# Sums on VectorE instead of GpSimd, four output chunks closed singly, and small matmuls planned later

## The chip, the cores and the metric

One core of one Trainium2 chip runs the whole program in one launch. The metric is device time in microseconds (us). The kernel before took 1167.01 us (median of 3 runs, 1165.86 to 1167.97). PE is the matmul engine (TensorE), DVE is VectorE, ACT is ScalarE, POOL is GpSimd, SP is the queue from which the weights are fetched.

## The reference, cut to what matters

The input is 256 tokens by 1024 features. Two transformer layers and one recurrent layer follow each other.

```python
for i in range(2):                                   # first_block
    h = x * (1.0 + sc_m) + sh_m                      # sc, sh, g: from c @ w_mod
    y = even_mixer(h, ...) if i == 0 else odd_mixer(h, ...)   # q, k: rotary; then out-projection
    x = layer_norm(ALPHA * x + (1.0 + g_m) * y, ln_mix_g[i], ln_mix_b[i])
    h = x * (1.0 + sc_f) + sh_f
    y = swiglu(h, w_gate[i], w_up[i], w_down[i])
    x = layer_norm(ALPHA * x + (1.0 + g_f) * y, ln_ffn_g[i], ln_ffn_b[i])
# second_block: rmsnorm, input projection, gated recurrence, out-projection,
# rmsnorm, convolved gated FFN, final rmsnorm
```

`layer_norm` needs the mean and the mean square over the 1024 features, `rmsnorm` the mean square. `apply_rope` is `t1*cos - t2*sin, t2*cos + t1*sin` on the two halves of each head. The even mixer has two kinds of attention, one of which first selects the 64 best keys of every query (`top_k`); the odd mixer is differential attention.

## The kernel before

**Layout.** Features lie on the 128 partitions, so an activation is 8 chunks of 128 x 256 (feature x token). Every weight is fetched in slabs of 128 x 2048 from SP's queue into `stage`. Each half of a slab (128 x 1024, one output chunk over all 8 input chunks) is rounded by ACT into `whi`, and DVE writes the rest `wlo = stage - whi`. An output chunk is then 8 x 3 matmuls of 128 x 256 (`mm3`): hi*hi, hi*lo, lo*hi. There are 6 buffers each of `whi` and `wlo`, and 8 PSUM banks.

**Order of the work.** Every instruction is recorded first (`Plan.record`) with an estimated cost, its dependences, and its place in the program (plus a bias) as its priority. `Plan.order` then plays the program through: on each engine it takes the ready instruction with the lowest priority number, where an instruction is ready when its inputs are, plus a hop of 300 ns if the input comes from another engine. The result is a fixed order on each engine, which the chip follows; an engine waits at an instruction whose input is late, and everything behind it waits too. The estimates for DVE and POOL don't depend on what the other one does.

**Layer norm over partitions** (`Norm`, used four times). `Norm.add(k, y)` takes output chunk k of a projection: DVE makes the residual `d` from PSUM, ACT and DVE make the split product `U[k]` (the input of the next projection, with the norm applied afterwards), ACT makes `sq = d*d`. POOL adds `d` and `sq` into two running totals s1 and s2 for k below `cut`. From k = cut on, the totals and then every single `d` and `sq` are summed over partitions by `column`: two f32 matmuls of one column each (one for each 128 tokens) against a vector of 1/1024. Each f32 matmul shows in the trace as two records. After k = 7 a few small DVE and ACT steps form the reciprocal root, and `spread` turns the two numbers of each token into a full 128 x 256 tile through four transposes on PE. The next projection's first four chunks (`group(norm.U, ..., outer=True)`, 96 matmuls over k in the outer loop) use `U`, so PE has them to do while the statistics are formed; the later chunks use `X`, which `ln_next` makes from the finished statistics (`ln_next`: two DVE steps, two ACT steps and one DVE step for each of the 8 chunks).

The norms behind the two mixers have cut=4, those behind the FFNs have cut=7. The fourth norm also carries three more totals (`add_sq`). `Rms` is the same with squares alone, twice in the last layer.

**Out-projection** (`out_proj`). It makes chunks 0 to 3 as one group with k in the outer loop, then the four `Norm.add`; then chunks 4 to 7 as a second group, one chunk behind the other, and then their four `Norm.add`.

**Rotary** (`rope_parts`). ACT copies the swapped quarters out of PSUM, DVE multiplies by the cosines, POOL multiplies the swapped copy by the signed sines, DVE adds.

Of the kernel before, what the change touches and what calls it, by code (L numbers as in the profile page):

```python
# [18 lines left out]
S = 256  # L19
# [29 lines left out]
for _l in range(2):  # L49
    for _p in (0, 3):  # L50
        MOD_ORDER += [(_l, _p + i, k) for k in range(8) for i in range(2)]
        MOD_ORDER += [(_l, _p + 2, k) for k in range(8)]

LAG = 300
XLAG = 600
BIAS = {'topk': 75, 'dsa': 75, 'sb': 0, 'diff': 0, 'diffo': -275, 'hgrn': 75, 'fetch': 0}
# [48 lines left out]
class Plan:  # L105
# [26 lines left out]
    def __init__(self, nc):  # L132
        self.ops = []
        self.hist = {}
        self.tiles = {}
        self.bufs = {}
        self.form = {}
        self.spare = {}
        self.bias = 0
        self.nc = nc  # L140
        self.vector = Plan.Engine(self, "DVE", nc.vector)
        self.scalar = Plan.Engine(self, "ACT", nc.scalar)
        self.gpsimd = Plan.Engine(self, "POOL", nc.gpsimd)
        self.tensor = Plan.Engine(self, "PE", nc.tensor)
        self.sync = Plan.Engine(self, "SP", nc.sync)
        self.aq = Plan.Engine(self, "AQ", nc.scalar)
        self.pq = Plan.Engine(self, "PQ", nc.gpsimd)
# [61 lines left out]
    def record(self, eng, op, fn, args, kw):  # L209
        writes, reads = [], []  # L210
        for i, a in enumerate(args):
            if isinstance(a, View):
                (writes if i == 0 else reads).append(a)
        for k, a in kw.items():
            if isinstance(a, View):
                (writes if k in ("out", "accum_out") else reads).append(a)
        idx = len(self.ops)
        deps = set()
        mine = []
        for lst, w in ((reads, False), (writes, True)):  # L220
            for a in lst:
                name = a.name
                b = self.box(a.sample)
                if self.tiles[name][1] is None:
                    assert w, (op, name)
                    self.tiles[name][1] = idx
                if idx not in self.tiles[name][2][-1:]:
                    self.tiles[name][2].append(idx)
                if name not in mine:
                    mine.append(name)  # L230
                h = self.hist.setdefault(name, [])
                keep = []
                for e in h:
                    j, ew, eb = e
                    over = eb[0] < b[1] and b[0] < eb[1] and eb[2] < b[3] and b[2] < eb[3]
                    if over and (w or ew) and j != idx:
                        deps.add(j)
                    if not (w and b[0] <= eb[0] and eb[1] <= b[1] and b[2] <= eb[2] and eb[3] <= b[3]):
                        keep.append(e)
                keep.append((idx, w, b))  # L240
                self.hist[name] = keep
        cost = self.cost(eng, op, [a.sample for a in writes], [a.sample for a in reads])
        need = self.SETS.get(args[2]) if op == "activation" else None
        work = 0.0
        if eng == "PE":
            work = 1.0
            for v in writes[0].shape[1:]:
                work *= v
            work *= reads[0].shape[0] / 128
            work *= 4 if reads[0].dtype == F32 and op == "matmul" else 2 if op == "transpose" else 1  # L250
        parts = 2 if len(writes) > 1 and eng == "ACT" or eng == "PE" and op == "matmul" and reads[0].dtype == F32 else 1
        self.ops.append((eng, fn, args, kw, cost, deps, mine, idx + self.bias, need, work, parts))

    def order(self):
        import heapq
        ops = self.ops
        n = len(ops)
# [26 lines left out]
        at = [0.0] * n  # L284
# [14 lines left out]
        while done < n:  # L299
            moved = False  # L300
            nxt = float("inf")
            for e in engs:
# [91 lines left out]
                        heapq.heappush(tags[self.tiles[nm][0]]["free"], (last[nm] + 100.0, slot[nm]))  # L394
                for j in succ[i]:
                    oj = ops[j]
                    at[j] = max(at[j], end + (self.SELF[e] if oj[0] == e else self.HOP))
                    need[j] -= 1
                    if not need[j]:
                        heapq.heappush(wait[oj[0]], (at[j], oj[7], j))  # L400
# [31 lines left out]
def kernel(ctx, tc, io, out):  # L432
# [269 lines left out]
    class Norm:  # L702
# [13 lines left out]
        def add(self, k, y):  # L716
            d = self.d[k]
            V.scalar_tensor_tensor(d, y, self.g1[:, k:k + 1], self.xa[k], op0=ALU.mult, op1=ALU.add)
            scale_split(self.U[0][k][:, :S], self.U[1][k][:, :S], d, self.lv[:, 16 + k:17 + k])
            sq = w1("lnq")[:, :S]  # L720
            A.activation(sq, d, AF.Square)
            if k == 0:
                self.q0 = sq
            elif k == 1:
                self.s1 = w1("lns1")[:, :S]
                self.s2 = w1("lns2")[:, :S]
                G.tensor_add(self.s1, self.d[0], d)
                G.tensor_add(self.s2, self.q0, sq)
            elif k < self.cut:
                G.tensor_add(self.s1, self.s1, d)  # L730
                G.tensor_add(self.s2, self.s2, sq)
            if self.sq:
                self.add_sq(k, d)
            if k >= self.cut:
                if k == self.cut:
                    self.p = bank("ps_s")
                    self.column(0, self.s1, first=True)
                    self.column(1, self.s2)
                self.column(0, d, last=k == 7)
                self.column(1, sq, last=k == 7)  # L740
            if k == 7:
                p = self.p
                if self.sq:
                    for c, a in enumerate((self.s3, self.s4, self.s5)):
                        self.column(2 + c, a, last=True)
                st = sm("st", 8)
                V.tensor_copy(st[:, 0:4], p[:, 0:4])
                V.tensor_mul(st[:, 4:6], st[:, 0:2], st[:, 0:2])
                V.tensor_sub(st[:, 4:6], st[:, 2:4], st[:, 4:6])
                root(st[:, 4:6], LN_EPS)  # L750
                V.tensor_mul(st[:, 6:8], st[:, 4:6], st[:, 0:2])
                self.r, self.mr = [bank("ps_b")[:, :S] for _ in range(2)]
                self.spread(self.r, st[:, 4:6])
                self.spread(self.mr, st[:, 6:8])
                self.rm = w2("rm")
                if self.sq:
                    self.root_sq(p[:, 4:10], st)
# [5 lines left out]
                         start=first and t == 0, stop=last, skip_group_check=True)  # L763

        def spread(self, dst, col):
            for t in range(2):
                T.transpose(dst[:, t * 128:t * 128 + 128], col[:, t:t + 1].to_broadcast([128, 128]), ident)

        def add_sq(self, k, d):

            g, gg, gb = [v[:, k:k + 1] for v in self.sq[:3]]
            sq = w1("lnq3")[:, :S]
            A.activation(sq, d, AF.Square, scale=g)
            if k == 0:
                self.q3 = sq
                self.s4 = w1("lns4")[:, :S]
                self.s5 = w1("lns5")[:, :S]
                V.tensor_scalar(self.s4, d, gg, None, op0=ALU.mult)
                V.tensor_scalar(self.s5, d, gb, None, op0=ALU.mult)
                return  # L780
            V.scalar_tensor_tensor(self.s4, d, gg, self.s4, op0=ALU.mult, op1=ALU.add)
            V.scalar_tensor_tensor(self.s5, d, gb, self.s5, op0=ALU.mult, op1=ALU.add)
            if k == 1:
                self.s3 = w1("lns3")[:, :S]
                G.tensor_add(self.s3, self.q3, sq)
            else:
                G.tensor_add(self.s3, self.s3, sq)

        def root_sq(self, p, st):

# [105 lines left out]
    def rope_parts(ps, n):  # L896
# [4 lines left out]
            s = q ^ 1  # L901
            A.activation(rot[q * 32:q * 32 + 32], ps[s * 32:s * 32 + 32], AF.Copy)
        V.tensor_mul(t1, ps, cosT[:, None, :].to_broadcast([128, n, S]))
        G.tensor_mul(rot, rot, sinT[:, None, :].to_broadcast([128, n, S]))
        return t1, rot


# [266 lines left out]
    mod_upto(40, LAG)  # L1174

    def out_proj(O, norm, korder):
        for s in range(2):
            pss = group(O, [ALLT] * 4, korder, outer=s == 0)
            for c in range(4):
                norm.add(4 * s + c, pss[c])  # L1180

    lv = ln_vectors(0, "lmg", "lmb", MV(0, 4, 0, 8), MV(0, 3, 0, 8))
    norm = Norm(xa, MV(0, 2, 0, 8), lv, cut=4)
    out_proj(O, norm, KORDER)

    def ffn_act(Gp, j, gate, up, bias=None):
# [134 lines left out]
    mod_upto(88, LAG)  # L1321

    lv = ln_vectors(1, "lmg", "lmb", MV(1, 4, 0, 8), MV(1, 3, 0, 8))
    norm = Norm(xa, MV(1, 2, 0, 8), lv, cut=4)
    out_proj(O, norm, ALLK)
    Gp, xa = ffn(norm, lv, 96)

# [46 lines left out]
    class Rms:  # L1374
# [7 lines left out]
        def add(self, h):  # L1382
# [7 lines left out]
            if i == 0:  # L1390
                self.acc = sq
            elif i == 1:
                a = w1("racc")[:, :n]
                G.tensor_add(a, self.acc, sq)
                self.acc = a
            elif i < self.cut:
                G.tensor_add(self.acc, self.acc, sq)
            if i >= self.cut:
                if i == self.cut:
                    self.p = bank("ps_s")  # L1400
# [459 lines left out]
```

## Time and profile before

| | |
|---|---|
| median of 3 runs | 1167.01 us |
| the profiled execution | 1165.6 us |
| its span, first to last instruction | 1163.8 us |
| PE busy | 1132.3 us, 97% |
| DVE busy | 910.6 us, 78% |
| ACT busy | 723.5 us, 62% |
| POOL busy | 88.2 us, 8% |
| mean granted PE clock | 0.988 |

The profiled execution lies 1.4 us under the median of the runs; 1.8 us of it lie outside the span. Matmuls overlap in the array, so the duration of one record (some 0.28 us) is longer than the distance from one start to the next (some 0.12 us for 256 columns); costs on PE are read from starts. All recorded instructions carry the same line, L428, since one helper issues them; they are told apart by their tiles: `pa` is PSUM, `w` any work tile, `cst` the constants, `sm` the small tiles, `mst` the modulation weights.

### The profile page before, as it was taken

Reading aid. Unit: us, or ns where it says so; the run is one execution under the profiler, and the core shown is the slowest. Engines: PE = TensorE matmul, PEld = TensorE weight load, DVE = VectorE, ACT = ScalarE, POOL = GpSimd, SP = SyncE. Lnnn points to the kernel's source line nnn. Section 1 sums busy time; section 2 is a strip of 40 time slices with the busy share of each in tenths; the row PEclk is TensorE's granted clock in tenths of the full one; section 3 lists DMA queues with packets and bytes.
Section 4 is the critical chain, followed back from the end, with each engine's and each line's share of the span. In section 5 each row is a group of like instructions: output and inputs, shape, how many; then the busy total and the mean of one; then the engine's idle time right before and its main releaser. Section 6 shows DMA issues by size and latency. Waiting matters only on the chain.

```text
span 1163.8 us, 22183 instructions
## 1 busy us (share of the span) xinstructions
PE 1132.3 (97%) x8835; PEld 1083.9 (93%) x8835; DVE 910.6 (78%) x1686; ACT 723.5 (62%) x1312; POOL 88.2 (8%) x84
## 2 busy tenths in 40 slices
PE   5999999999999899999999999999999999999997
PEld 4885899999999778999999999999999999999996
DVE  6799899888999999865557886996669887866642
ACT  3558676445449887764455558786767865655541
POOL 0110200000231302000003400000000010000011
PEclk9999989999999999899999999999999999999998
DMA  9938758988995333455554634344433424555441
GB/s 353 409 131 309 240 196 319 337 325 305 335 335 191 114 129 126 145 218 184 187 191 168 228 110 158 130 148 179 155 117 131 178 87 171 195 188 193 169 163 37
DMA packets 42247, 232.28 MB, mean 200 GB/s; under 512 B 4640, under 2 KB 6176, under 8 KB 24096
## 3 DMA queue, kind: packets, MB, share of 16 engines
q1 hardware_dynamic: 42144, 230.87, 55.0%
q8 instruction: 69, 1.13, 0.4%
q14 instruction: 34, 0.28, 0.1%
HBM read 229.81 MB, written 1.05 MB: 198 GB/s over the span
## 4 chain that ended last, share of the span: by engine, by line
PE 85%; DVE 7%; DMA 3%; ACT 3%; issue 1%; DVEq 0%; SPq 0%; ACTq 0%
PE pa L428 85%; DVE w L428 4%; ACT w L428 2%; DVE wlo L428 2%; DMA mst<-in_wmod_dram 1%; DVE sm L428 1%; DVE mst L428 1%; DMA whi<-in_w_dram 1%; DMA cst<-in_cst_dram 1%; ACT whi L428 1%; DMA vec<-in_vecs_dram 0%; ACT sm L428 0%; ACT scb L428 0%; DVE lnv0lmg L428 0%; DVEq L1856 0%
## 5 line engine op out<-in xcount | busy, mean ns | idle before, releaser
L428 PE MATMUL pa<-w,whi 128*128 128x256 f32 (+4 forms) x5104 | 914.5, 287 | 9.6 <-DMA whi<-in_w_dram 7.5
L428 PEld LDWEIGHTS pa<-w,whi 128*128 128x128 f32 x5104 | 766.9, 190 | 17.0 <-ACT w L428 7.6
L428 PE MATMUL pa<-w,wlo 128*128 128x256 f32 (+3 forms) x2608 | 659.5, 289 | 0.0
L428 ACT ACTIVATE whi<-stage 128x1024 fp32r<-128x1024 f32 (+1 forms) x330 | 340.2, 1042 | 257.2 <-PE pa L428 233.9
L428 DVE TENSOR_TENSOR wlo<-stage,whi 128x1024 fp32r<-128x1024 f32 (+1 forms) x330 | 401.4, 1226 | 110.1 <-ACT whi L428 104.5
L428 PEld LDWEIGHTS pa<-w,wlo 128*128 128x128 f32 x2608 | 464.0, 190 | 7.7 <-issue 4.0
L428 ACT ACTIVATE w<-w 128x256 fp32r<-128x256 f32 (+9 forms) x257 | 117.6, 470 | 74.0 <-DVE w L428 70.3
L428 ACT ACTIVATE w<-pa 128x256 f32<-128x256 f32 (+12 forms) x298 | 108.3, 391 | 40.9 <-PE pa L428 36.1
L428 DVE TENSOR_TENSOR w<-w,w 128x256 fp32r<-128x256 f32 (+7 forms) x263 | 120.1, 474 | 8.0 <-ACT w L428 5.1
L428 DVE SCALAR_TENSOR_TENSOR mst<-mst,scb 128x1024 f32<-128x1024 f32 x90 | 109.5, 1226 | 10.8 <-DMA mst<-in_wmod_dram 10.6
L428 DVE TENSOR_TENSOR w<-w,pa 128x256 f32<-128x256 f32 (+2 forms) x146 | 58.9, 417 | 57.3 <-PE pa L428 52.3
L428 POOL TENSOR_TENSOR w<-w,w 128x256 f32<-128x256 f32 (+1 forms) x50 | 56.5, 1150 | 527.5 <-ACT w L428 320.7
L427 ACT ACT_TABLE_LOAD x59 | 75.7, 1283 | 1.7 <-PEq L1850 0.7
L428 PE MATMUL pa<-w,w 128*128 128x128 f32 (+8 forms) x340 | 70.0, 331 | 1.7 <-DVE w L428 1.1
L428 PEld LDWEIGHTS pa<-w,w 128*128 128x128 f32 (+4 forms) x340 | 41.4, 171 | 11.5 <-issue 4.1
L428 PE MATMUL pa<-cst,w 128*128 128x1 f32 (+4 forms) x284 | 46.5, 265 | 3.6 <-DVE w L428 2.2
L428 PEld LDWEIGHTS pa<-cst,w 128*128 128x128 f32 (+2 forms) x284 | 36.0, 175 | 12.0 <-ACT w L428 4.5
L428 POOL TENSOR_TENSOR w<-w 128x256 f32<-128x256 f32 x4 | 3.2, 799 | 415.2 <-DVE w L428 415.2
L428 PE MATMUL pa<-w 128*128 128x128 f32 x240 | 34.6, 274 | 0.0
L428 PE MATMUL pa<-whi,w 128*128 128x512 f32 x96 | 32.5, 417 | 0.2 <-ACT w L428 0.2
L428 PEld LDWEIGHTS pa<-w 128*128 128x128 f32 x240 | 31.2, 191 | 0.0
L428 DVE SCALAR_TENSOR_TENSOR w<-pa,vec,w 128x256 f32<-128x256 f32 (+1 forms) x48 | 23.1, 482 | 6.7 <-PE pa L428 5.7
(145 smaller groups left out, 537.1 us busy)
## 6 DMA issues: line engine op xcount, KB each, us to landing
mst<-in_wmod_dram SPq DMA_DIRECT2D x90, 512.0 KB, 5.4
stage<-in_wgu_dram SPq DMA_DIRECT2D x44, 1024.0 KB, 4.9
stage<-in_wi_dram SPq DMA_DIRECT2D x36, 1024.0 KB, 4.8
stage<-in_wup_dram SPq DMA_DIRECT2D x22, 1024.0 KB, 4.8
stage<-in_wd_dram SPq DMA_DIRECT2D x24, 896.0 KB, 4.7
stage<-in_w_dram SPq DMA_DIRECT2D x15, 1024.0 KB, 6.2
stage<-in_wo_dram SPq DMA_DIRECT2D x12, 1024.0 KB, 4.8
stage<-in_wd_dram SPq DMA_DIRECT2D x12, 1024.0 KB, 4.8
```

The source lines that it names most:

```text
L427: self.nc.scalar.preload_act_table_set(tables[i])
L428: fn(*[real(a) for a in args], **{k: real(a) for k, a in kw.items()})
```

## The change

It has five parts.

1. The running totals of `Norm` (s1, s2, and s3 in `add_sq`) and of `Rms` are added on VectorE (`V`) instead of GpSimd (`G`), and so is the sine product of `rope_parts`.
2. The norms behind the mixers get the default cut=7: the totals run over k = 0 to 6, and only k = 7 is summed by itself.
3. In `Norm.add` the column sums of the totals, and of the three extra totals, are recorded at k = 7, ahead of those of `d` and `sq`.
4. `out_proj` still makes chunks 0 to 3 as a group; chunks 4 to 7 are made one at a time, each followed by its own `Norm.add`.
5. A constant HOLD = 800 ns: while `Norm` records column sums or the transposes of `spread`, the planner takes inputs from another engine to be 800 ns later than otherwise. This alters the planned order only; no wait is added to the program itself.

```diff
+HOLD = 800.0
@@ Plan.record
+        if self.hold:
+            self.late[idx] = self.hold
@@ Plan.order
-                    at[j] = max(at[j], end + (self.SELF[e] if oj[0] == e else self.HOP))
+                    at[j] = max(at[j], end + (self.SELF[e] if oj[0] == e else self.HOP + self.late.get(j, 0.0)))
@@ Norm.add
-                G.tensor_add(self.s1, self.d[0], d)
-                G.tensor_add(self.s2, self.q0, sq)
+                V.tensor_add(self.s1, self.d[0], d)
+                V.tensor_add(self.s2, self.q0, sq)
             elif k < self.cut:
-                G.tensor_add(self.s1, self.s1, d)
-                G.tensor_add(self.s2, self.s2, sq)
+                V.tensor_add(self.s1, self.s1, d)
+                V.tensor_add(self.s2, self.s2, sq)
...
             if k >= self.cut:
+                run.hold = HOLD
                 if k == self.cut:
                     self.p = bank("ps_s")
-                    self.column(0, self.s1, first=True)
+                if k == 7:
+                    self.column(0, self.s1, first=self.cut == 7)
                     self.column(1, self.s2)
-                self.column(0, d, last=k == 7)
+                    if self.sq:
+                        for c, a in enumerate((self.s3, self.s4, self.s5)):
+                            self.column(2 + c, a, last=True)
+                self.column(0, d, first=k == self.cut < 7, last=k == 7)
                 self.column(1, sq, last=k == 7)
+                run.hold = 0.0
@@ Norm.spread
+            run.hold = HOLD
             for t in range(2):
                 T.transpose(dst[:, t * 128:t * 128 + 128], col[:, t:t + 1].to_broadcast([128, 128]), ident)
+            run.hold = 0.0
@@ Norm.add_sq (twice) and Rms.add (twice): G.tensor_add becomes V.tensor_add
...
@@ rope_parts
-        G.tensor_mul(rot, rot, sinT[:, None, :].to_broadcast([128, n, S]))
+        V.tensor_mul(rot, rot, sinT[:, None, :].to_broadcast([128, n, S]))
@@ out_proj
-        for s in range(2):
-            pss = group(O, [ALLT] * 4, korder, outer=s == 0)
-            for c in range(4):
-                norm.add(4 * s + c, pss[c])
+        pss = group(O, [ALLT] * 4, korder, outer=True)
+        for c in range(4):
+            norm.add(c, pss[c])
+        for c in range(4, 8):
+            norm.add(c, group(O, [ALLT], korder)[0])
@@ both mixers' norms
-    norm = Norm(xa, MV(0, 2, 0, 8), lv, cut=4)
+    norm = Norm(xa, MV(0, 2, 0, 8), lv)
```

## Rows read from the trace of the kernel before

**Rows 1.** The page: the span, and busy time, share and instructions of three engines.
```profile
span 1163.8 us, 22183 instructions
PE 1132.3 (97%) x8835; PEld 1083.9 (93%) x8835; DVE 910.6 (78%) x1686; ACT 723.5 (62%) x1312; POOL 88.2 (8%) x84
```

**Rows 2.** Whole-run waits of PE: for whom, us in total, times, longest us.
```profile
PE pa L428 <- ACT w L428: 3.8, 9, 1.4
PE pa L428 <- DVE w L428: 3.7, 5, 1.6
...
PE pa L428 <- DVE biasb L428: 1.9, 1, 1.9
PE pa L428 <- DVE sm L428: 1.8, 2, 1.1
```

**Rows 3.** Timeline of PE, first mixer's norm: start, us, what, [idle before].
```profile
148.61 4.55 PE L428 MATMUL pa<-cst,w 128*128 128x1 f32 x40
...
157.05 1.11 PE L428 MATMUL pa<-cst,sm 128*128 128x128 f32 x4 [1.08 <-DVE sm L428]
...
168.87 0.40 PE L428 MATMUL pa<-w,whi 128*128 128x256 f32 x2
```

**Rows 4.** Timeline of PE, second mixer's norm.
```profile
469.12 6.55 PE L428 MATMUL pa<-cst,w 128*128 128x1 f32 x40
...
490.22 0.40 PE L428 MATMUL pa<-w,whi 128*128 128x256 f32 x2
```

**Rows 5.** Windows: us, busy (x) of PE, PEld, DVE, ACT, POOL; PEclk; DMA.
```profile
155.00:160.00 5.00, 3.92 (x19) 3.62 (x19) 4.72 (x16) 2.98 (x6) 0.00 (x0) 0.50 0.86 290
...
345.00:350.00 5.00, 5.00 (x44) 5.00 (x44) 4.90 (x11) 2.47 (x5) 0.00 (x0) 1.00 0.89 324
...
475.00:480.00 5.00, 5.00 (x25) 5.00 (x25) 1.90 (x9) 2.29 (x5) 0.00 (x0) 0.50 0.76 313
```

**Rows 6.** Chain of waits: start, us, what; one unbroken piece on PE.
```profile
853.62 300.46 PE pa L428 x2496
```

**Rows 7.** Timeline of PE at the first FFN's norm (cut=7).
```profile
344.64 0.95 PE L428 MATMUL pa<-cst,w 128*128 128x1 f32 x8
...
346.58 0.50 PE L428 MATMUL pa<-cst,w 128*128 128x1 f32 x4
```

**Rows 8.** Groups by shape, whole run: count | busy us, mean ns | idle before.
```profile
L428 POOL TENSOR_TENSOR w<-w,w 128x256 f32<-128x256 f32 x47 | 53.3, 1156 | 248.1 <-issue 159.0 <-DVE w L428 47.6 <-ACT w L428 41.5
...
L428 DVE TENSOR_TENSOR w<-w,w 128x512 f32<-128x512 f32 x49 | 32.6, 686 | 1.4 <-ACT w L428 1.4
...
L428 DVE TENSOR_TENSOR w<-w,w 128x256 f32<-128x256 f32 x42 | 17.4, 430 | 0.7 <-ACT w L428 0.2
...
L428 POOL TENSOR_TENSOR w<-w,sinT 128x512 f32<-128x512 f32 x9 | 12.7, 1409 | 53.2 <-ACT w L428 45.7 <-DVE w L428 7.6
...
L428 POOL TENSOR_TENSOR w<-w,sinT 128x256 f32<-128x256 f32 x5 | 5.4, 1074 | 54.6 <-ACT w L428 54.5
```

**Rows 9.** Groups on DVE by shape, 137.5 to 146 us, POOL adding beside it.
```profile
L428 DVE TENSOR_TENSOR wlo<-stage,whi 128x1024 fp32r<-128x1024 f32 x3 | 4.2, 1397 | 0.0
L428 DVE SCALAR_TENSOR_TENSOR w<-w,lnv0lmg,w 128x256 fp32r<-128x256 f32 x4 | 3.7, 960 | 0.0
L428 DVE SCALAR_TENSOR_TENSOR w<-pa,mod,w 128x256 f32<-128x256 f32 x4 | 1.7, 478 | 0.0
```

**Rows 10.** The same groups, 149 to 155 us, POOL idle.
```profile
L428 DVE TENSOR_TENSOR wlo<-stage,whi 128x1024 fp32r<-128x1024 f32 x3 | 3.6, 1207 | 0.0
L428 DVE SCALAR_TENSOR_TENSOR w<-w,lnv0lmg,w 128x256 fp32r<-128x256 f32 x4 | 1.9, 468 | 0.0
```

**Rows 11.** Windows, columns as in Rows 5: first out-projection's end; differential attention.
```profile
137.00:149.00 12.00, 12.00 (x105) 12.00 (x103) 12.00 (x17) 9.34 (x18) 6.74 (x6) 1.00 0.47 155
...
365.00:412.00 47.00, 42.94 (x296) 36.32 (x294) 44.90 (x87) 42.91 (x96) 13.95 (x11) 1.00 0.38 135
```

**Rows 12.** Timeline of PE behind the fourth norm.
```profile
685.68 0.50 PE L428 MATMUL pa<-w,whi 128*128 128x258 f32 x2 [0.25 <-ACT w L428]
```

More of the change, by code (lines that the diff above doesn't have):

```diff
@@ L139, in __init__ @@
         self.bias = 0
+        self.hold = 0.0
+        self.late = {}
         self.nc = nc
@@ L734, in add @@
             if k >= self.cut:
+                run.hold = HOLD
                 if k == self.cut:
                     self.p = bank("ps_s")
-                    self.column(0, self.s1, first=True)
+                if k == 7:
+                    self.column(0, self.s1, first=self.cut == 7)
                     self.column(1, self.s2)
-                self.column(0, d, last=k == 7)
+                    if self.sq:
+                        for c, a in enumerate((self.s3, self.s4, self.s5)):
+                            self.column(2 + c, a, last=True)
+                self.column(0, d, first=k == self.cut < 7, last=k == 7)
                 self.column(1, sq, last=k == 7)
+                run.hold = 0.0
             if k == 7:
                 p = self.p
-                if self.sq:
-                    for c, a in enumerate((self.s3, self.s4, self.s5)):
-                        self.column(2 + c, a, last=True)
                 st = sm("st", 8)
@@ L784, in add_sq @@
                 self.s3 = w1("lns3")[:, :S]
-                G.tensor_add(self.s3, self.q3, sq)
+                V.tensor_add(self.s3, self.q3, sq)
             else:
-                G.tensor_add(self.s3, self.s3, sq)
+                V.tensor_add(self.s3, self.s3, sq)
         def root_sq(self, p, st):
@@ L1323 @@
     lv = ln_vectors(1, "lmg", "lmb", MV(1, 4, 0, 8), MV(1, 3, 0, 8))
-    norm = Norm(xa, MV(1, 2, 0, 8), lv, cut=4)
+    norm = Norm(xa, MV(1, 2, 0, 8), lv)
     out_proj(O, norm, ALLK)
@@ L1393, in add @@
                 a = w1("racc")[:, :n]
-                G.tensor_add(a, self.acc, sq)
+                V.tensor_add(a, self.acc, sq)
                 self.acc = a
             elif i < self.cut:
-                G.tensor_add(self.acc, self.acc, sq)
+                V.tensor_add(self.acc, self.acc, sq)
             if i >= self.cut:
```

## Prediction

> **What bounds the kernel now.** I read the page first. PE is busy for 1132.3 of 1163.8 us, DVE for 910.6 [rows 1]; so time is won where PE stands still, runs slowly, or does work that can go, and the rest of the program can at best be hidden. PE's waits come second [rows 2]: those that ACT or DVE end add up to 3.8 + 3.7 + 1.9 + 1.8 = 11.2 us, a third of the 31.5 us that PE is idle; the reader is to see that no single wait is large. Third, PE's timeline at the two norms behind the mixers, since the diff takes PE work away there. From the end of the out-projection PE does 40 column records in one burst, then 96 matmuls of the next projection with four transpose records among them. That takes 148.61 to 168.87, 20.26 us, in the first layer [rows 3], and 469.12 to 490.22, 21.10 us, in the second [rows 4]. The windows show why it is so long: after the burst the granted clock is 0.50, the lower of the two levels (1.2 against 2.4 GHz) [rows 5]. In an undisturbed piece PE starts a matmul every 300.46 / 2496 = 0.120 us [rows 6], so the 96 need 11.5 us at the full clock.
>
> **The change part by part.** The sum is made against the profiled execution, 1165.6 us, which is 1.4 us under the median.
>
> *Column sums.* With cut=4 each mixer norm has (2 + 8) columns of two token halves, each two records: 40, as the rows show. With cut=7 there are 4 x 2 x 2 = 16. The 24 that go cost 4.55 / 40 = 0.114 us each in the first layer, 2.7 us; in the second, where the clock falls during the burst, 6.55 / 40 = 0.164 us.
>
> *The clock behind them.* An FFN norm has 16 records already, in pieces of 8, 4 and 4 with matmuls between [rows 7], and the clock stays at 1.00 around them [rows 5]. I therefore take the mixer norms to keep the full clock as well. Each stretch then needs 16 x 0.114 = 1.8, four transpose records at half of their slow-clock 1.11, say 0.6, and 11.5 us: 13.9. Against 20.26 and 21.10 that is 6.3 and 7.2 us less, in which the 1.08 us wait before the first norm's transposes is included: the later place in the order puts some 0.8 / 0.12 = 7 matmuls into it. What bounds it: the columns alone (2.7 each) if the slow clock comes back, the whole if nothing is late.
>
> *Sums on DVE.* POOL's sums number 45 of the 47 [rows 8], plus four first ones and three of 258 columns; 52 move, and the two mixer norms get six more each. At 0.43 us each, the 64 put 27.5 us on DVE, and the 14 sine products 9 x 0.69 + 5 x 0.43 = 8.4 us: 35.9 in all. Against that stands what POOL does to DVE now. While POOL adds, the split product takes 960 ns and `wlo` 1397 [rows 9]; a few us later, with POOL idle, the same two take 468 and 1207 [rows 10]. Four of the one and three of the other are 2.0 + 0.6 = 2.6 us lost beside six sums, 0.43 for each: as much as the sum will cost on DVE. So I count the moved sums at nothing and only the new ones, 6 x 0.43 = 2.6 us in each mixer norm.
>
> In [rows 9] the product that reads PSUM does not suffer: 478 ns beside POOL. The Trainium skill, "SBUF — State Buffer", section "Who interferes with whom", has the same line: a VectorE instruction with two SBUF inputs and a GpSimd instruction that reads SBUF block each other outright. By that rule the exchange is even, and the trace agrees.
>
> *Who waits for the new sums.* In the first layer DVE is full at that place, 12.00 of 12 us [rows 11], so the transposes, at 157.05 now, can come 2.6 later, at 159.7. From there to the first normalised chunk there are five steps of DVE and ACT, at 0.43 to 0.69 us like the rows of their size: 161.9 to 163.2. PE is through its 96 matmuls at 148.61 + 13.9 = 162.5. Behind the first chunk each of the others follows in three DVE steps, 1.3 us, while PE needs 12 x 0.120 = 1.4. I charge 1.0 us here (bounds 0 and 2.6), nothing in the second layer, where DVE is busy for only 1.90 of the 5 us from 475 [rows 5]. So the norms give -5.3 and -7.2.
>
> *Chunks 4 to 7 singly.* PE's matmuls are the same in number and in order. What moves are the `Norm.add` of chunks 4 to 6, ahead of the fetches and `wlo` splits of the next weights in priority; SP's queue keeps its order. Six buffers each of `whi` and `wlo` hold two chunks in reserve, 2 x 24 x 0.120 = 5.8 us of PE. A `wlo` of 1.2 us that stands behind two more sums is 0.9 us late: hidden, 0; without the reserve it would be 0.9 for each of three chunks.
>
> *Sine products.* In differential attention DVE is busy for 44.90 of 47 us and PE idle for 47 - 42.94 = 4.1 [rows 11]. Ten products fall there, six long and four short: 5.8 us. POOL time cost DVE 2.6 / (6 x 1.156) = 0.37 us per us above; ten products of 1.409 and 1.074 are 12.8 us of POOL, so 4.7 come back: +1.1 net. Each product itself ends earlier, 0.69 for 1.41. Between all idle gone (-4.1) and the net load in full (+1.1) I take the middle, -1.5; the outer bound is +5.8, no relief. The first mixer has the other four, 2.5 us on DVE with 2.0 back, ahead of the key selection for which PE waits 1.9 [rows 2]: I take 0 (bounds -1.9 and +2.5).
>
> *The planned delay.* PE does other matmuls meanwhile, 96 of them at each norm. Only behind the fourth norm is the cover seen to end: PE waits 0.25 us for a normalised chunk [rows 12]. Columns, transposes and the extra transposes may each come 0.8 later; I charge one, +0.8 (bounds 0 and 2.4). `Rms` is not delayed, and its sums move at no price like the others.
>
> Sum: -5.3 - 7.2 - 1.5 + 0 + 0.8 = -13.2; 1152.4 for this execution, 1153.8 beside the median.
>
> **The rivals.** *The slow clock stays.* The order is fixed, and the two totals are now the last sums of a full DVE; if they come later than planned, PE stands at their columns with the 96 matmuls behind it, and the stretch ends slow again. For it: DVE has no idle time at 137 to 149. Against it: POOL's slowing of DVE, which the planner didn't know, goes, so its times fit better. Then only columns are saved, 2 x 2.7 less the 0.8: 1165.6 - 4.6 = 1161.0, or 1162.4 beside the median.
>
> *Everything late vanishes.* The same better fit could empty PE's waits in attention too: -6.3 - 7.2 - 4.1 - 1.9 = -19.5, 1147.5. For it: five waits on DVE of 3.7 us in all [rows 2]. Against it: DVE is at 96% there.
>
> *VectorE becomes the bound: slower.* If the slowing beside POOL was no loss to DVE (time that it would have waited for ACT or PE anyway), every moved operation counts in full where DVE is full: 12 x 0.43 in each mixer norm, 5.8 and 2.5, together 18.6 us, against PE's 13.5. That is +5.1, 1170.7, or 1172.1 beside the median. It decides once less than 5.1 of the 18.6 come back. For it: DVE's share of the three stretches; against it: DVE stands without gaps beside POOL, so what it lost was work time.
> The Trainium skill speaks for this rival in "Perfetto Trace Analysis", section "Optimizing Scalar/DVE Operations": with VectorE saturated, handing work to ScalarE or even GpSimd may make sense, and the change does the reverse; the same paragraph doubts it for these two, since they share a port, and the doubled product above bears out the doubt.
>
> **How the numbers follow.** Forecast 0.60 (own range 1149 to 1159, from the bounds of the norms' 1.0 and 0.8 and of attention), slow clock 0.20, everything vanishes 0.12, VectorE as the bound 0.08. A new plan also moves small waits elsewhere by a few us either way. The range 1146 to 1164 takes in the first three. About 0.2%, 2.3 us, is what a measurement can tell: faster 0.85 (nearly all of the first three), same 0.08 (the slow clock with an unlucky plan), slower 0.07.
>
> **What would show it.** Right: 16 column records per mixer norm with matmuls between them, PE's clock at 1.00 after the out-projections, about 14 us from its last matmul to the first 128x256 matmul of the FFN; the split product at 0.47 us throughout; DVE's busy time up by under 10 us and not by 36. Wrong: a clock of 0.50 there, PE idle before column or transpose records, DVE up by the full 36, or longer waits on `w` and `biasb` in the two attention stretches.

## The result and the profile after

| | before | changed |
|---|---|---|
| median of 4 runs | 1167.31 us (1165.86 to 1167.97) | 1157.97 us (1156.16 to 1161.21) |
| profiled execution, span | 1165.6, 1163.8 us | 1161.2, 1159.4 us |
| ratio | | 0.9921 [0.9906, 0.9937] |

A second set of the same two kernels, on another chip, gave 1157.14 us (6 runs) against 1168.11, 0.9908 [0.9891, 0.9925]. The forecast was 1153.8; the time lies 3 to 4 us above it and inside the range.

The page of the changed kernel, against [rows 1]:

```profile
span 1159.4 us, 21967 instructions
PE 1127.6 (97%) x8787; PEld 1079.3 (93%) x8787; DVE 912.1 (79%) x1764; ACT 723.1 (62%) x1314; POOL 12.4 (1%) x18
```

VectorE has 78 instructions more and is busy for only 1.5 us more (910.6 before), where their durations were estimated to add up to some 36. POOL has next to nothing left. What paid for the sums is seen in the groups on DVE by shape, 137.5 to 146 us of the changed kernel, against [rows 9] (count | busy us, mean ns | idle before):

```profile
L433 DVE TENSOR_TENSOR w<-w,w 128x256 f32<-128x256 f32 x5 | 1.9, 421 | 0.1
L433 DVE SCALAR_TENSOR_TENSOR w<-w,lnv0lmg,w 128x256 fp32r<-128x256 f32 x4 | 1.8, 482 | 0.0
L433 DVE TENSOR_TENSOR wlo<-stage,whi 128x1024 fp32r<-128x1024 f32 x1 | 1.2, 1219 | 0.0
```

The split product is back from 960 to 482 ns and `wlo` from 1397 to 1219. By the Trainium skill, "SBUF — State Buffer", section "Who interferes with whom", a VectorE instruction with two SBUF inputs and a GpSimd instruction that reads SBUF shut each other out; the trace agrees, 960 ns with POOL adding and 482 without. That the exchange comes out even is read from the measured times alone.

PE's timeline at the two mixer norms, against [rows 3] and [rows 4] (start, us, what, [idle before]). First the first layer, then the second:

```profile
145.39 0.51 PE L433 MATMUL pa<-w,whi 128*128 128x258 f32 x2 [0.32 <-ACT whi L433]
...
151.64 0.50 PE L433 MATMUL pa<-cst,w 128*128 128x1 f32 x4
...
153.34 0.50 PE L433 MATMUL pa<-cst,w 128*128 128x1 f32 x4
...
154.16 0.50 PE L433 MATMUL pa<-cst,w 128*128 128x1 f32 x4
...
154.84 0.50 PE L433 MATMUL pa<-cst,w 128*128 128x1 f32 x4
...
159.13 0.60 PE L433 MATMUL pa<-cst,sm 128*128 128x128 f32 x4
...
164.50 0.40 PE L433 MATMUL pa<-w,whi 128*128 128x256 f32 x2
...
464.36 0.50 PE L433 MATMUL pa<-cst,w 128*128 128x1 f32 x4
...
471.83 0.60 PE L433 MATMUL pa<-cst,sm 128*128 128x128 f32 x4
...
477.16 0.40 PE L433 MATMUL pa<-w,whi 128*128 128x256 f32 x2
```

Sixteen column records in four pieces, matmuls between them, no idle time ahead of columns or transposes. (The second layer's other three pieces, at 466 to 468 us, are left out.) From the end of the out-projection, at 151.16 and 463.88, the stretches take 164.50 - 151.16 = 13.3 us and 477.16 - 463.88 = 13.3, against 20.26 and 21.10 before. Four of the 96 matmuls of the next projection (128x258 in the rows) have run by then: in the new order they stand among those of the out-projection, at 144.67 to 145.61 and 458.18 to 458.54. With them, 4 x 0.12 = 0.5, both stretches take 13.8 us. The windows of the changed kernel (columns as in [rows 5]) show the clock at 1.00 there. In the window of differential attention DVE is busy for 3.1 us less than in [rows 11]; the changed kernel is 3 to 4 us ahead there, so the window's ends hold other work. Between the same matmuls (2200 to 2600 by the numbers below) DVE is busy for 85.6 us before and 80.4 after.

```profile
155.00:160.00 5.00, 5.00 (x45) 5.00 (x44) 4.86 (x11) 2.59 (x4) 0.00 (x0) 1.00 0.80 270
475.00:480.00 5.00, 5.00 (x44) 4.96 (x43) 4.93 (x15) 4.91 (x12) 0.00 (x0) 1.00 0.42 175
365.00:412.00 47.00, 41.94 (x275) 34.49 (x274) 41.80 (x95) 43.43 (x97) 0.00 (x0) 1.00 0.35 123
```

Where the time went can be followed by numbering the matmuls that read `whi` or `wlo` (7856 in each trace) and comparing the starts of the same number. The table gives the change over each stretch in us, minus for time gained, against the profiled execution of before. The third column is the changed kernel profiled a second time (span 1155.2 us), the last the kernel before profiled a second time (span 1162.8).

```
stretch (matmul numbers)                        predicted  changed  again  before again
start to the last of the out-projection (500)        0      +2.1    +2.8     +1.0
norm of mixer 1 and its 96 (500 to 608)            -6.3     -6.4    -6.5     -2.3
behind it (608 to 800)                             +1.0     +0.9    +0.9      0.0
differential attention (2200 to 2600)              -1.5     -2.2    -2.1      0.0
norm of mixer 2 and its 96 (2600 to 2864)          -7.2     -7.3    -7.3     -1.6
behind it (2864 to 3000)                             0      +0.9    +0.9      0.0
fourth norm (4200 to 4600)                         +0.8     +2.8    +1.2     +0.1
recurrent layer to its first Rms (4600 to 6200)      0      +3.1    +1.5     +1.6
first Rms to the end (6200 to 7800)                  0      +2.1    +0.1     +0.1
sum, with the stretches left out (0.2 at most)    -13.2    -4.4    -8.7     -1.0
```

The last column shows how much of such a table is nothing but two executions of one program: up to 2.3 us in a stretch. Most of it is clock. The second execution of before lost less at its norms, and some in the recurrent layer, where the first had lost nothing. The clock is also most of the gain: in the second set the mean granted clock of the runs is 0.987 before and 0.993 after, which is 0.006 x 1160 = 7 of the 11 us by this estimate.

### The profile page after: what moved, and what is told of

It is laid out like the page before. It is cut to its first block, busy times and chain, and to the rows that moved or that the text cites. A ratio compares the mean times of both kernels' runs of the same rounds, so it can differ in the third digit from the quotient of the medians.

```text
span 1159.4 us, 21967 instructions
## 1 busy us (share of the span) xinstructions
PE 1127.6 (97%) x8787; PEld 1079.3 (93%) x8787; DVE 912.1 (79%) x1764; ACT 723.1 (62%) x1314; POOL 12.4 (1%) x18
## 3 DMA queue, kind: packets, MB, share of 16 engines
q8 instruction: 69, 1.13, 0.4%
## 4 chain that ended last, share of the span: by engine, by line
PE 82%; DVE 9%; ACT 5%; DMA 3%; issue 1%; SPq 0%; DVEq 0%; ACTq 0%
PE pa L433 82%; DVE w L433 5%; ACT w L433 4%; DMA mst<-in_wmod_dram 2%; DVE wlo L433 2%; DVE mst L433 1%; ACT whi L433 1%; DVE sm L433 1%; DMA w<-in_pos_dram 1%; DMA w<-in_xT_dram 1%; DVE stage L433 0%; SPq L433 0%; ACT sm L433 0%; DVE mw L433 0%; DVEq L1867 0%
## 5 line engine op out<-in xcount | busy, mean ns | idle before, releaser
L433 DVE TENSOR_TENSOR wlo<-stage,whi 128x1024 fp32r<-128x1024 f32 (+1 forms) x330 | 392.8, 1201 | 93.1 <-ACT whi L433 90.8
L433 DVE TENSOR_TENSOR w<-w,w 128x256 fp32r<-128x256 f32 (+6 forms) x323 | 144.8, 465 | 10.9 <-ACT w L433 9.0
L433 PE MATMUL pa<-cst,w 128*128 128x1 f32 (+4 forms) x236 | 38.8, 255 | 3.3 <-ACT w L433 3.3
L433 PEld LDWEIGHTS pa<-cst,w 128*128 128x128 f32 (+2 forms) x236 | 29.0, 158 | 10.0 <-ACT w L433 6.1
L433 DVE SCALAR_TENSOR_TENSOR w<-pa,mod,w 128x256 f32<-128x256 f32 x32 | 15.0, 481 | 14.8 <-PE pa L433 14.8
L433 DVE COPY_PREDICATED w<-msk,pa 128x512 f32<-128x512 uint8 x28 | 20.5, 737 | 3.9 <-PE pa L433 3.8
```

Of the source, the lines that this page charges most:

```text
L433: fn(*[real(a) for a in args], **{k: real(a) for k, a in kw.items()})
```

## The experiments

All ratios are to the kernel before on the same chip.

**Fewer records, everything else as changed.** The two mixer norms get their four separate chunks back.

```diff
-    norm = Norm(xa, MV(0, 2, 0, 8), lv)          # and MV(1, 2, 0, 8)
+    norm = Norm(xa, MV(0, 2, 0, 8), lv, cut=4)
```

> The changed kernel with one part undone: both mixer norms again sum single d and sq columns from k = 4 on (40 column records each, 24 more than the changed kernel has). Records-and-clock theory: the gain of the change sits in the two mixer norms and comes from fewer column records and from PE keeping its full clock behind them. The records alone are 2 x 24 x 0.114 = 5.5 us, so some 1163.5 us if the later planned place spreads the columns between matmuls and the clock stays at 1.00; if they run in a burst and the clock falls to 0.50 as in the kernel before, 4 to 5 us more, about 1168. Rival theory (VectorE's relief): the gain comes from taking GpSimd off VectorE's port, and the number of columns hardly matters: within 2 us of the changed kernel's 1158.0.

1162.67 us, 0.9956 [0.9938, 0.9973]: 4 to 6 us of the gain (0.9956 against 0.9921 and 0.9908) are the 2 x 24 records, 5.5 us at 0.114. Its windows at the same two places show something that I had wrong:

```profile
155.00:160.00 5.00, 5.00 (x43) 5.00 (x44) 4.86 (x12) 1.84 (x3) 0.00 (x0) 1.00 0.93 328
...
470.00:475.00 5.00, 5.00 (x43) 5.00 (x43) 4.86 (x12) 3.11 (x5) 0.00 (x0) 1.00 0.80 316
```

Forty records leave the clock at 1.00 as well when they come in fours and eights between matmuls, as they do here. So the smaller number is not needed for it. Over all profiles of these experiments: at the 16 mixer norms of the eight profiles where the records come in pieces of at most twelve and PE doesn't stand before them, the clock is 1.00 throughout; behind bursts of 32 to 40 it fell in five of six cases. That the spreading keeps the clock fits this, though one burst without a fall shows that a burst alone does not decide it.

**The totals back on GpSimd, everything else as changed.** All 64 sums of `Norm`, `add_sq` and `Rms`; the sine products stay on VectorE.

```diff
-                V.tensor_add(self.s1, self.s1, d)    # and the seven others
+                G.tensor_add(self.s1, self.s1, d)
```

> The changed kernel with the running totals of Norm and Rms back on GpSimd (the sine products stay on VectorE). Records-and-clock theory: a sum on GpSimd costs VectorE 0.43 us by blocking, as much as doing it; so within 2 us of 1158.0, the two mixer norms perhaps 1 us later each because twelve sums at 1.16 us are 13.9 us long behind 8 chunks. Rival theory (VectorE's relief makes the gain): 5 us or more slower, 1163 to 1168, with PE waits before the column records.

1167.41 us, 0.9998 [0.9986, 1.0009]: the whole gain is gone, which my theory had excluded and the rival had forecast, with the waits. But DVE has no more to do by it: with 64 instructions fewer it is busy for 913.5 us, against 912.1 in the changed kernel. What the sums cost on DVE they cost it on POOL too. The page of this kernel, then POOL's timeline, then PE's at both norms, then two windows:

```profile
PE 1129.9 (97%) x8787; PEld 1081.8 (93%) x8787; DVE 913.5 (78%) x1700; ACT 724.9 (62%) x1314; POOL 84.0 (7%) x82
```
```profile
140.31 12.45 POOL L433 TENSOR_TENSOR w<-w,w 128x256 f32<-128x256 f32 x11 [0.44 <-ACT w L433]
```
```profile
151.94 0.60 PE L433 MATMUL pa<-cst,w 128*128 128x1 f32 x4 [1.72 <-POOL w L433]
...
471.14 0.60 PE L433 MATMUL pa<-cst,w 128*128 128x1 f32 x4 [1.76 <-POOL w L433]
```
```profile
155.00:160.00 5.00, 5.00 (x24) 5.00 (x24) 3.83 (x10) 1.80 (x3) 0.00 (x0) 0.50 0.65 241
475.00:480.00 5.00, 5.00 (x30) 5.00 (x30) 3.67 (x9) 1.49 (x2) 0.00 (x0) 0.65 0.60 210
```

With cut=7 the totals take in three chunks more, and at 12.45 / 11 = 1.13 us a sum POOL ends too late: PE stands 1.7 us at each norm's first columns, and behind that the clock falls, though the records come in pieces of four. By the numbered matmuls the two norms gain 1.4 and 2.2 us instead of 6.4 and 7.3, so nearly the whole loss lies there.

**One part alone, from the kernel before.** First only the longer totals (cut=7 at the mixer norms, sums on GpSimd), then only the move (sums and sine products on VectorE, cut=4, old order of the columns, no planned delay).

```diff
-    norm = Norm(xa, MV(0, 2, 0, 8), lv, cut=4)   # and MV(1, 2, 0, 8)
+    norm = Norm(xa, MV(0, 2, 0, 8), lv)
```

> The kernel before with cut=7 in the two mixer norms alone: sums stay on GpSimd, out-projection and planned times as before. Theory that fewer records need VectorE's sums to pay: GpSimd needs some 12.4 us for twelve sums (as in the run with its sums put back), ends after the last square, PE waits 1.7 us before the columns and its clock falls as before; only records are saved, 5.5 us less the two waits of 1.7: 1164 to 1167 beside 1167.3 for the kernel before. Rival (the records alone make the gain): 11 to 12 us faster, 1155 to 1157.

```diff
-                G.tensor_add(self.s1, self.s1, d)    # and the seven others, and the sine product
+                V.tensor_add(self.s1, self.s1, d)
```

> The kernel before with the running totals and the sine products on VectorE, and nothing else: cut=4, second out-projection group as before, no planned delay. Same theory: the 40 column records still run in one burst and the clock falls behind it, so the mixer norms gain nothing; attention gains its 2 us: 1165 to 1167. Rival (VectorE's relief is the whole gain): 8 to 10 us faster, 1157 to 1160.

The longer totals alone: 1166.48 us, 0.9993 [0.9984, 1.0002], as the theory had it. The same wait as above, longer; PE's timeline and a window of that kernel:

```profile
152.06 1.00 PE L428 MATMUL pa<-cst,w 128*128 128x1 f32 x4 [2.85 <-POOL w L428]
...
470.85 0.61 PE L428 MATMUL pa<-cst,w 128*128 128x1 f32 x4 [2.09 <-POOL w L428]
```
```profile
155.00:160.00 5.00, 5.00 (x28) 5.00 (x29) 3.61 (x11) 1.49 (x2) 0.00 (x0) 0.61 0.57 213
```

The move alone: 1162.21 us, 0.9960 [0.9942, 0.9978], between the two expectations; its runs spread from 1157.18 to 1166.93. Its PE timeline and windows:

```profile
144.47 0.95 PE L428 MATMUL pa<-cst,w 128*128 128x1 f32 x8
...
150.81 3.63 PE L428 MATMUL pa<-cst,w 128*128 128x1 f32 x32
...
466.44 3.85 PE L428 MATMUL pa<-cst,w 128*128 128x1 f32 x34
```
```profile
155.00:160.00 5.00, 5.00 (x33) 5.00 (x33) 4.36 (x11) 2.98 (x6) 0.00 (x0) 0.71 0.82 265
470.00:475.00 5.00, 4.62 (x39) 4.40 (x38) 4.58 (x13) 2.74 (x5) 0.00 (x0) 1.00 0.68 224
```

Now 8 and 6 records stand ahead of the bursts. Behind one of the remaining bursts the clock fell, behind the other, which is longer, it did not. That also accounts for most of the spread of the runs: those of 1157.18 to 1159.42 us had a mean granted clock of 0.993, those of 1166.90 and 1166.93 one of 0.986, and 0.007 x 1162 = 8 of the 10 us between them. The two parts hang together: the longer totals alone bring under 1 us, and taking them out of the changed kernel costs 4 to 6; the move alone brings 5, and taking its sums out costs all 9 to 11. All parts but the planned delay, in the next run, bring 7.

**The planned delay.** First HOLD = 0 everywhere; then no delay at the fourth norm alone, which is where I had charged it.

```diff
-HOLD = 800.0
+HOLD = 0.0
```

> The changed kernel with the planned delay set to 0 (HOLD = 0); all else stays. Theory: the delay gathers all twenty last column records of the fourth norm into one burst (658.65 us in the changed kernel's trace), 3.4 us after the last square, and the clock falls behind it; that costs 2.6 us there, which come back, while the two mixer norms keep theirs, since 16 records are too few to matter: 1155 to 1156. Rival: the delay is what keeps PE from standing before late columns; without it PE waits 1 to 2 us before columns or transposes at each of the four norms: 1161 to 1165, with longer waits of PE on sm and w.

```diff
-                run.hold = HOLD                          # and in spread
+                run.hold = 0.0 if self.sq else HOLD      # self.sq: the fourth norm
```

> The changed kernel with the planned delay kept at the first three norms and taken away at the fourth alone (the one with three extra totals). Theory that the delay costs the fourth norm a burst and 1.6 us of lateness: 2 to 3 us faster than the changed kernel, 1155 to 1156, with the clock at 1.00 from 655 to 670 us and the columns in several pieces. Rival: the fourth norm is late because its sums now stand in VectorE's queue; then nothing changes, 1158.0 within 1 us, and the columns still start about 2 us after the last square.

Without any delay 1161.72 us, 0.9942 [0.9926, 0.9958]; without it at the fourth norm alone 1156.41, 0.9900 [0.9883, 0.9916]. On the same chip that is 5.3 us for the delay at the first three norms, a constant that I had counted as a cost; its absence at the fourth is not told from the changed kernel, whose intervals overlap. My theory is out. The rival had the time but not the mechanism: PE does not stand at the columns or transposes. It stands behind the 96 matmuls, in the next group. PE's waits from 455 to 495 us without the delay:

```profile
PE pa L433 <- ACT whi L433: 0.7, 1, 0.7
PE pa L433 <- DVE w L433: 0.4, 2, 0.2
PE pa L433 <- DVE wlo L433: 0.3, 1, 0.3
```

and the same stretch with the delay at the first three norms:

```profile
PE pa L433 <- DVE wlo L433: 0.2, 1, 0.2
```

By numbered matmuls (400 to 800, 2600 to 3000) the two mixer norms with what lies around them gain 3.8 and 4.0 us without any delay, and 4.8 and 6.5 where only the fourth norm is without. Up to the last of the 96 (608 and 2864) the two kernels agree within 0.1 us; the difference of 1.0 and 2.4 lies behind. That is 3.5 of the 4.9 us between these two profiled spans (1160.3 and 1155.4). Why a later planned place of the transposes leads to fewer late inputs is not shown: it changes the order on all engines. At the fourth norm (4200 to 4600) the cost is +1.2 us in the second profile of the changed kernel, the same with no delay there, and the same with none anywhere. It is of the size that I charged, but not the delay's. Nor is it the place of the sums: the kernel with the move alone loses 0.1 us there. What the kernels that lose have in common is the new order of the columns (part 3 of the change): PE's timeline there without any delay, then with the move alone,

```profile
662.52 2.29 PE L433 MATMUL pa<-cst,w 128*128 128x1 f32 x20
```
```profile
662.60 1.40 PE L428 MATMUL pa<-cst,w 128*128 128x1 f32 x12
```

With the new order the columns come in pieces of 8 and 20; with the old one in pieces of 8, 4, 4 and 12, as in the kernel before. No run takes this part away alone, so the cause is likely and not shown.

**Chunks 4 to 7 as a group again.**

```diff
-        pss = group(O, [ALLT] * 4, korder, outer=True)
-        for c in range(4):
-            norm.add(c, pss[c])
-        for c in range(4, 8):
-            norm.add(c, group(O, [ALLT], korder)[0])
+        for s in range(2):
+            pss = group(O, [ALLT] * 4, korder, outer=s == 0)
+            for c in range(4):
+                norm.add(4 * s + c, pss[c])
```

> The changed kernel with chunks 4 to 7 of the out-projection as one group again and their norm steps recorded behind it. Theory: the single closing only moves priorities; PE's matmuls are the same, and the 16 column records stay 16: within 1.5 us of 1158.0. Rival: only with single closing does VectorE get through the sums of chunks 4 to 6 while PE still multiplies; without it PE waits before the columns, the clock falls again, and 4 to 6 us are lost: 1162 to 1164.

1158.29 us, 0.9929 [0.9916, 0.9942]: the interval overlaps both sets of the changed kernel, so in the time closing the chunks singly is worth nothing that can be told, as predicted. By the numbered matmuls (500 to 800, 2600 to 3000) the two norms gain 5.0 and 5.0 us without it and 5.6 and 6.5 in the changed kernel, in both profiles within 0.1: some 2 us, in what stands behind the 96 matmuls above all.

**The sine products back on GpSimd, everything else as changed.**

```diff
-        V.tensor_mul(rot, rot, sinT[:, None, :].to_broadcast([128, n, S]))
+        G.tensor_mul(rot, rot, sinT[:, None, :].to_broadcast([128, n, S]))
```

> The changed kernel with the sine products of the rotary step back on GpSimd. Theory: they are worth the 2 us that differential attention gained (PE's progress 3.6 us ahead at its start, 5.7 ahead at its end), so 1159 to 1161. Rival (VectorE is at its limit there, 44.9 of 47 us, and each product costs it): 1 to 3 us faster, 1155 to 1157.

1158.94 us, 0.9932 [0.9920, 0.9945]: 1 to 3 us slower than the changed kernel by the ratios, with overlapping intervals, so not told from nothing. What it shows lies in differential attention (2200 to 2600). That stretch gains 2.0 us in this kernel too, 2.2 in the changed one, and 2.7 in the kernel with nothing but cut=7, though POOL makes all ten products there in both. POOL's groups from 365 to 446 us with the products back on it:

```profile
L433 POOL TENSOR_TENSOR w<-w,sinT 128x512 f32<-128x512 f32 x6 | 10.6, 1772 | 49.6 <-ACT w L433 49.6
L433 POOL TENSOR_TENSOR w<-w,sinT 128x256 f32<-128x256 f32 x4 | 5.0, 1264 | 6.8 <-ACT w L433 6.8
```

So the gain in attention is not the place of the product. It comes with the new orders that these edits bring, the longer totals by themselves included; what in the order does it is not shown.

**A version that goes further.** The rows of the changed kernel point to one more burst. At the first `Rms`, PE's timeline has

```profile
953.33 3.41 PE L433 MATMUL pa<-cst,w 128*128 128x1 f32 x30
...
958.98 0.93 PE L433 MATMUL pa<-cst,sm 128*128 128x128 f32 x3 [0.44 <-DVE sm L433]
```

and the window behind it a low clock:

```profile
960.00:965.00 5.00, 5.00 (x25) 5.00 (x26) 4.55 (x13) 3.14 (x9) 0.00 (x0) 0.54 0.45 187
```

The same three edits are made there (cut=7, chunks 4 to 7 closed singly, the delay), and the fourth norm stays without its delay.

```diff
-    rms = Rms(NR, VC("fnw", 0, 8), cut=4)
+    rms = Rms(NR, VC("fnw", 0, 8))        # columns and transposes of it under HOLD
-    for s in range(2):
-        for c, ps in enumerate(group(M, [slice(0, NR)] * 4, outer=s == 0)):
+    for c, ps in enumerate(group(M, [slice(0, NR)] * 4, outer=True)):
+        close(c, ps)                      # residual, then rms.add
+    for c in range(4, 8):
+        close(c, group(M, [slice(0, NR)])[0])
```

> The changed kernel with two further edits: no planned delay at the fourth norm (as in the run before), and the first rms norm treated like the mixer norms: its totals run to the seventh chunk (12 column records instead of 30), chunks 4 to 7 of its out-projection are closed singly, and its columns and transposes are planned 800 ns later. Records-and-clock theory: 18 x 0.114 = 2.1 us of records, and the 1.7 to 3.4 us that the clock falls behind this burst in every profile so far come back: 3 to 5 us faster than the run without the fourth norm's delay (1156.4), so 1151.5 to 1153.5, the clock at 1.00 from 945 to 965 us. Rival: behind this norm nothing covers the later statistics, so PE waits before the transposes instead: 1155 to 1157.

1153.18 us, 0.9876 [0.9857, 0.9896], as the theory had it and the fastest of the kernels; on that chip the changed one took 1157.14. From the first `Rms` to the end (6200 to 7800) it gains 3.4 us against the kernel before, where the changed kernel loses 0.1 in its second profile. Its PE timeline and window:

```profile
952.19 0.66 PE L433 MATMUL pa<-cst,w 128*128 128x1 f32 x6
...
953.59 0.65 PE L433 MATMUL pa<-cst,w 128*128 128x1 f32 x6
```
```profile
960.00:965.00 5.00, 5.00 (x44) 5.00 (x43) 4.32 (x13) 3.56 (x8) 0.00 (x0) 1.00 0.29 121
```

**Both kernels profiled again**, for the last two columns of the table above and for what two executions of one program differ by.

> The changed kernel as it is, once more. It tells whether the three clock falls that its first profile shows away from the mixer norms (661, 715 and 848 us, 1.7 us each) belong to the change or to the single execution. If to the change: the same three at the same places, and 1161 again in the profiled execution. If they come by chance: falls at other places or fewer, the profiled execution between 1156 and 1160; the one behind the first rms norm's burst of 30 records near 957 stays in either case.

> The kernel before, once more, for a second profile. If falls of the clock in the recurrent layer come by chance, they can show here as well, near 722 and 853 us, where its first profile has none; those behind the two bursts of 40 records should be there again, at about 154 and 471 us, 3.4 to 5.1 us each in lost time at the half clock.

Of the changed kernel's falls those at 661 and 848 us belong to the one execution: the second (1156.96 us) hasn't them, and has one at 118 us instead. Those at 715 us and behind the first `Rms` stand in both. In the kernel before both bursts were again followed by a fall, but a shorter one (1.7 and 3.4 us lost, where the first profile has 3.4 and 5.1), and one more stands at 853 us, none near 722.

The fourth norm of the changed kernel, in its first profile and then in its second, one window of each:

```profile
660.00:665.00 5.00, 5.00 (x30) 5.00 (x30) 2.29 (x16) 0.41 (x2) 0.00 (x0) 0.66 0.19 79
```
```profile
660.00:665.00 5.00, 5.00 (x43) 5.00 (x43) 2.29 (x16) 0.41 (x2) 0.00 (x0) 1.00 0.34 139
```

The same order, the same DVE and ACT work, and in one of them a third of the clock is missing: 0.34 x 5 = 1.7 us.

## Why the prediction was right, and where it was not

*Column sums and clock: right, for a reason that was half right.* Both stretches were to take 13.9 us and took 13.8 with the four matmuls that ran earlier; -6.4 and -7.3 stand where -6.3 and -7.2 were forecast. But 16 records do not keep the clock by themselves: behind a wait it falls all the same, and 40 spread ones keep it too.

*Sums on DVE at nothing: right in DVE's time, too narrow in its scope.* Busy time rose by 1.5 us, and putting the 64 sums back lowers it by nothing, so the VectorE rival was rightly given little. But I treated cut=7 as a gain by itself and the move as an even exchange. The runs show the reverse dependence: cut=7 gains nothing while POOL adds (1.7 to 2.9 us of waiting at each norm's columns, then the low clock), and the move alone gains 5. The step left out who must deliver the seventh sum, and when.

*What the new sums hold up.* Behind the first norm +0.9 for the charged 1.0. Behind the second +0.9 where I charged nothing. With cut=4 and all else as changed it is +0.3 behind each, so some 0.6 is the new sums'. I had read DVE's free time (1.90 of 5 us busy, [rows 5]) inside the slow stretch. In the changed kernel the stretch ends at 477, and DVE is busy for 4.93 of the 5 us from 475.

*First mixer at nothing: the largest miss in the table.* To the end of the out-projection the changed kernel loses 2.1 to 2.8 us, of which an execution of before loses up to 1.0 by itself. The wait for key selection did shrink; PE's waits of the changed kernel from 60 to 148 us show what took its place (in [rows 2] `biasb` had 1.9), and below them the only such wait on DVE or ACT in the same stretch of the kernel with the sine products back on GpSimd:

```profile
PE pa L433 <- DVE w L433: 2.3, 2, 1.2
PE pa L433 <- ACT w L433: 1.5, 1, 1.5
PE pa L433 <- DVE biasb L433: 0.3, 1, 0.3
```
```profile
PE pa L433 <- DVE biasb L433: 1.9, 1, 1.9
```

Two waits on DVE and one on ACT, 2.3 and 1.5 us, stand where `biasb` stood. They come with the four sine products on VectorE, and not with the sums: the kernel with the sums back on GpSimd and the products on VectorE has them too (2.4 and 1.5 us). The net of these waits, some 2.2 us, is near the +2.5 that I gave as the bound. One of them is a split of an attention output behind a modulation product of 1.23 us, in DVE's and PE's timelines:

```profile
123.21 1.23 DVE L433 SCALAR_TENSOR_TENSOR mst<-mst,scb 128x1024 f32<-128x1024 f32 x1
...
124.36 0.42 DVE L433 TENSOR_TENSOR w<-pa,w 128x256 fp32r<-128x256 f32 x1
```
```profile
124.83 0.50 PE L433 MATMUL pa<-w,whi 128*128 128x256 f32 x2 [1.03 <-DVE w L433]
```

*Sine products: right number, wrong cause.* -2.2 for -1.5 in attention, but kernels that leave the product on POOL have the same gain; what the products' place does change is the first mixer, above.

*The planned delay: wrong sign.* Charged at +0.8, it is worth some 3.5 us at the mixer norms. This is where the forecast had luck: without the delay the two norms gain 4.6 and 4.0 us (matmuls 500 to 800, 2600 to 3000), where 5.3 and 7.2 were forecast, and the kernel takes 1161.7 us. The gain that made up for it came from the part that I had priced as a cost.

*What is missing.* In the second profile the gain is 4.5 us short of the 13.2: 2.8 in the first mixer, 0.8 behind the two norms, 1.5 in the recurrent layer where the clock fell at 715 us, and 0.5 at the fourth norm and the end, against 0.9 more than forecast at the norms themselves and in attention. The base plays a part: the execution on which the sum rests had lost 2.3 and 1.6 us more at its norms than its second profile (the table's last column), so that much of the norms' term was that execution's own. The rival of the slow clock (1162.4) is out, since the clock is 1.00 at both norms; that in which everything late vanishes (1147.5) is out by the new waits in the first mixer.

## What to carry to other kernels

When an accumulation is lengthened, ask first which engine delivers its last sum: here the longer totals gained nothing on GpSimd, the move alone 0.4%, both with the rest 0.8 to 0.9%, of which 0.2 to 0.4% hang on the planned delay. Small matmuls that wait for statistics are better put in pieces between large ones: at the mixer norms no stretch in pieces without a wait lost its clock, and most with a burst did. Before a gain at a low clock is counted, profile the kernel twice: the low stretches of two executions of one program need not agree.

## What the runs showed of the hardware

TensorE's clock also falls away from the norms, in some executions of a program and not in others. In the recurrent layer 12 one-column matmuls of 0.54 us in all stand at 850 us; behind them PE has one gap, of 0.2 us, and is then busy throughout. The kernel before at 855 to 860 us, in its second profile and then in its first:

```profile
855.00:860.00 5.00, 5.00 (x37) 5.00 (x36) 3.08 (x4) 2.75 (x4) 0.00 (x0) 0.81 0.01 2
```
```profile
855.00:860.00 5.00, 5.00 (x42) 4.88 (x42) 2.96 (x5) 3.29 (x5) 0.00 (x0) 1.00 0.39 165
```

Such falls recur near the same places (660, 715, 850 and 957 us) in several kernels, all four of them only in the first profile of the changed one, two in its second; the one behind the first `Rms` in every profile but that of the last version. Single ones stand elsewhere: near 82 us with the sine products back, 118 in the second profile of the changed kernel, 128 with chunks 4 to 7 as a group, 392 without any delay, 410 with the longer totals alone. No run here shows what decides.
